# Merging the hi and lo halves of the moving operand into one wide matmul instruction in a float32 two-layer trunk

## The chip, the cores and the metric

One NeuronCore of a Trainium2 chip runs the whole kernel. The metric is device time of one execution in microseconds (us), the median of three runs. Engines are named as in the profile: PE (TensorE matmul), PEld (TensorE weight load), DVE (VectorE), ACT (ScalarE), POOL (GpSimd), SP (SyncE, which issues the transfers).

## The reference

A sequence of 256 tokens of 2048 features gets 16 meta tokens in front (272 in all, L) and runs through two layers, each `h <- h + norm(mixer(norm(h)))`. Layer 0 is differential attention with 8 heads: four projections (q, k, v and a gate), two score maps for each head (head dimension 128), two softmaxes over the allowed keys, `a = p1 - lam * p2`, values of 256 features, a norm for each head, a product with `silu(gate)`, an output projection. The queries are treated in three blocks: the 16 meta tokens (16 keys), the first 128 tokens (144 keys) and the second 128 tokens (272 keys). Layer 1 is a pooling mixer: a projection to u and a gate, causal window means of u minus u, a product with a 512 by 512 matrix in each of four feature groups (the mixing), a scale, a product with `silu(gate)`, an output projection. Everything is float32.

## The kernel before

Features lie on the 128 partitions and tokens along the free dimension. To hold float32 accuracy, each operand of a product is split in two float32r halves, hi (rounded) and lo (the exact rest). A product w x is then three matmuls that accumulate in one PSUM bank, `mm3` (lines 118 to 122): w_hi x_hi (L120), w_hi x_lo (L121), w_lo x_hi (L122), each with a weight load of its own. In the profile the weights are the stationary operand, and x's columns are the moving one.

Weights come as chunks of 128 by 2048 (1 MiB). `split` (L96 on ACT, L97 on DVE) makes hi and lo of a chunk; three places for each are in turn. One chunk of 128 output features is a *slot*: 16 contraction tiles, 48 matmuls (`proj`). In layer 0 the slots are q, q, k, k, v, v of each head, then 16 gate chunks. A head's attention runs between the projections of the next head, ordered by `after_proj`: at that head's first slot `scores` and `v_turn` (for head 0 a slot later, slot 7, and there ahead of the evacuation of the slot's own product), at its third `a_turn`, at its fourth `values`, at its fifth `sums` (L423, L424: sums of squares over partitions by a matmul with ones). In the fourth slot `qk_split` (L296 to L300) works on the same engines as the ending of `values`.

In `scores`, block 1 (first 128 queries, 144 keys) puts both maps in one bank and block 2 uses a bank for each map. DVE masks in place, takes the maximum, and ACT takes the exponential from PSUM (L377). In `values`, a bank gets one product for the meta keys (L411), an `mm3` of 256 columns and an `mm3` of 128 columns for the last key tile; ACT then squares (L414) and scales (L415) it, DVE adds the two squares (L416), ACT and DVE split the sum (L418, L419), and `sums` reads that.

In layer 1, `mixing` (L634) runs 16 `mm3` of 256 columns for each of four chunks, evacuated by one ACT instruction (L642). The 16 gate chunks (tile `pv`) are 16 `mm3` each of 256 columns, and `gate1` reads the bank with one DVE product (L646), then silu, product, split to zh and zl (L650). The output projection (tile `pz`) uses zh and zl as the stationary operand and 512 columns of weights as the moving one.

PSUM is one pool of eight banks for everything; a product waits until a bank is free. The order of instructions on an engine is fixed when the kernel is built, by a planner that goes by order in the program and by when it reckons an operand is ready; `tc.issue_after` adds a few orders by hand. The trace shows that it is not the bare program order: DVE's mask of block 1 (L371) stands among the small sums of block 0 (L346 to L348).

Of the kernel before, what the change touches and what calls it, by code (L numbers as in the profile page):

```python
# [42 lines left out]
def trunk(ctx: ExitStack, tc: tile.TileContext, hT, small, gpost1, rope, w_in, w_out, p_in, p_grp, p_out, out):  # L43
# [58 lines left out]
    def fold(f, o):  # L102
        """o = the sum of the KT tiles in f, which doesn't stay."""
# [14 lines left out]
    def mm3(o, wh, wl, xh, xl, first, last):  # L118
        """o += w^T x with both operands split; the product of the two low halves lies below float32's rounding."""
# [60 lines left out]
    xl = base.tile([P, KT, L], F32R, tag="xl", name="xl")  # L180
    oh = base.tile([P, KT, L], F32R, tag="oh", name="oh")
    ol = base.tile([P, KT, L], F32R, tag="ol", name="ol")
# [9 lines left out]
    # The first chunks run along with the loads of x, tile by tile.  # L192
# [63 lines left out]
    # Rope with the norm's factor in it: rp[:, 0] = r0 cos (1 beyond the rotated rows), rp[0:32, 1] = -+ r0 sin.  # L256
# [7 lines left out]
    # lambda = exp(q1 k1) - exp(q2 k2) + lambda_init, on every partition  # L264
# [7 lines left out]
    # sub-norm gain times (1 - lambda_init)  # L272
# [3 lines left out]
    def proj(ps, n0, n1, rh, rl, mid=None):  # L276
        """A chunk of 128 output features: ps[:, 0:n1-n0] over the tokens n0..n1."""
# [12 lines left out]
    def qk_evac(hd, i, ps):  # L290
        """i: q1, q2, k1, k2. Norm and the rope's cosine part; the swapped rows aside."""
# [13 lines left out]
    # The meta keys in one product: blocks of 32 partitions with v's (hi, hi, lo) against the weights' (hi, lo, hi);  # L305
    # the last 16 partitions of a block stay zero.
# [5 lines left out]
    def v_turn(hd):  # L312
        """v with the keys on the partitions, split; the norm's factor goes in here."""
# [18 lines left out]
    def scores(hd):  # L332
        """Softmaxes of both maps and their difference, by query block: hd.a[block], queries on the partitions."""
        h = hd.h
        hd.a = []
        for b, (q0, q1) in enumerate(TOK):
            nk, nq = q1, q1 - q0
            if b == 0:
                # Both maps' (hi, lo) queries against their (hi, lo) keys in one product, of which these parts count.
# [22 lines left out]
            mx = att.tile([P, 2], F32, name=f"mx{h}_{b}", tag=f"mx{b}")
            if b == 0:
# [10 lines left out]
            e = att.tile([P, 2, nk], F32, name=f"e{h}_{b}", tag=f"e{b}")  # L374
# [11 lines left out]
    def a_turn(hd):  # L386
        """The weights with the keys on the partitions, split."""
# [8 lines left out]
        hd.th = att.tile([P, 384], F32R, name=f"th{h}", tag="th")  # L396
        hd.tl = att.tile([P, 384], F32R, name=f"tl{h}", tag="tl")
# [6 lines left out]
    def values(hd):  # L404
        """The head's output, features on the partitions, and its squares."""
        h = hd.h
        hd.sq = att.tile([P, 2, L], F32, name=f"sq{h}", tag="e2")
        for j in range(2):
# [4 lines left out]
            mm3(po[:, 144:272], hd.vh[:, 1, s], hd.vl[:, 1, s], hd.th[:, 256:384], hd.tl[:, 256:384], False, True)  # L413
# [25 lines left out]
    def after_proj(slot, ps):  # L439
# [61 lines left out]
        # VectorE splits the next chunk before it turns to this one's products.  # L501
# [19 lines left out]
    for m in range(KT):  # L521
# [7 lines left out]
        if m >= KT - 5:  # L529
            # The next layer's first chunks run side by side: one more place for them.  # L530
# [34 lines left out]
    for n in (1, 1, 2, 2, 2, 2, 2, 2, 2):  # L565
        # h += norm(y) g; times the next norm's gain, split.
# [36 lines left out]
    # residual with the tokens on the partitions  # L603
# [198 lines left out]
```

## Time and profile before

| what | value |
|---|---|
| three runs | 852.3, 852.71, 853.0 us; median 852.71 |
| span of the profiled execution, first to last instruction | 850.4 us |
| median less that span | 2.3 us |
| granted TensorE clock, mean | 0.998 of full |
| PE busy | 838.5 us (99%), 6498 matmuls |
| DVE busy | 563.7 us (66%) |
| ACT busy | 420.9 us (49%) |
| DMA | 147.31 MB, mean 173 GB/s |
| chain that ended last | PE 96%, waiting for nothing shown 1%, the rest 1% or less each |

The time of the profiled execution is not listed apart from the three runs; what lies around its span is taken as the 2.3 us between span and median. A matmul's duration in the profile (some 280 ns for 256 columns) includes its way through the array, and matmuls overlap; what one costs in a row is the distance between the starts of two. The same holds for weight loads.

### The profile page before, as it was taken

The numbers are of one execution on the slowest core, as the hardware profiler recorded it, in microseconds if no ns is written. First come the engines' busy times: TensorE is split into PE (matmuls) and PEld (weight loads), VectorE is DVE, ScalarE is ACT, GpSimd is POOL, SyncE is SP. The second block draws the span as 40 slices with busy tenths as digits, with TensorE's granted clock in tenths as the row PEclk, the third lists the DMA queues.
The fourth block names the chain that finished last, engine by engine and source line by source line (L and its number), as shares of the span: only waits on it lengthen the run. The fifth ranks groups of instructions, "written<-read, shape, count | busy, mean of one in ns | idle before, by whom it ended". The sixth has DMA issues, their size and how long they took to land.

```text
span 850.4 us, 15239 instructions
## 1 busy us (share of the span) xinstructions
PE 838.5 (99%) x6498; PEld 823.1 (97%) x6498; DVE 563.7 (66%) x873; ACT 420.9 (49%) x617; POOL 5.4 (1%) x16
## 2 busy tenths in 40 slices
PE   8999999999999999999999999999999999999996
PEld 7999999999999999999999999999999999998896
DVE  6689676676758586977854454787767665574423
ACT  7556545454545455855343444554544444453420
POOL 0000000000000000000000000000000000000000
PEclk9999999999999999999999999999999999999999
DMA  8645444444444444445457546154575455546512
GB/s 298 218 158 190 149 149 150 150 148 162 144 179 149 161 149 150 149 153 194 155 199 298 198 153 241 54 201 151 193 249 188 164 195 198 178 169 202 194 50 99
DMA packets 24435, 147.31 MB, mean 173 GB/s; under 512 B 2736, under 2 KB 4528, under 8 KB 7856
## 3 DMA queue, kind: packets, MB, share of 16 engines
q1 hardware_dynamic: 24368, 146.34, 49.4%
q8 instruction: 51, 0.84, 0.4%
q14 instruction: 16, 0.13, 0.0%
HBM read 144.23 MB, written 2.10 MB: 172 GB/s over the span
## 4 chain that ended last, share of the span: by engine, by line
PE 96%; issue 1%; DMA 1%; DVE 1%; ACT 0%; SPq 0%; DVEq 0%; POOLq 0%; POOL 0%; ACTq 0%
PE p L120 14%; PE p L121 14%; PE p L122 14%; PE py L121 4%; PE py L120 4%; PE py L122 4%; PE pu L121 4%; PE pu L122 4%; PE pu L120 4%; PE pv L121 4%; PE pv L122 4%; PE pv L120 4%; PE pz L698 3%; PE pz L696 3%; PE pz L697 3%
## 5 line engine op out<-in xcount | busy, mean ns | idle before, releaser
L97 DVE TENSOR_TENSOR lo<-raw,hi 128x2048 fp32r<-128x2048 f32 (+1 forms) x126 | 281.8, 2238 | 156.2 <-ACT hi L96 155.9
L96 ACT CAST hi<-raw 128x2048 fp32r<-128x2048 f32 (+1 forms) x126 | 235.0, 1868 | 214.1 <-PE p L121 80.4
L120 PE MATMUL p<-xh,hi 128*128 128x272 f32 x944 | 274.2, 290 | 0.0
L121 PE MATMUL p<-xl,hi 128*128 128x272 f32 x944 | 273.1, 289 | 0.0
L122 PE MATMUL p<-xh,lo 128*128 128x272 f32 x944 | 272.6, 289 | 0.0
L120 PEld LDWEIGHTS p<-xh,hi 128*128 128x128 f32 x944 | 177.9, 188 | 0.0
L122 PEld LDWEIGHTS p<-xh,lo 128*128 128x128 f32 x944 | 177.7, 188 | 0.0
L121 PEld LDWEIGHTS p<-xl,hi 128*128 128x128 f32 x944 | 177.6, 188 | 0.0
L121 PE MATMUL py<-ol,hi 128*128 128x272 f32 x256 | 74.3, 290 | 0.0
L122 PE MATMUL py<-oh,lo 128*128 128x272 f32 x256 | 73.8, 288 | 0.0
L120 PE MATMUL py<-oh,hi 128*128 128x272 f32 x256 | 73.7, 288 | 0.0
L121 PE MATMUL pv<-hl,hi 128*128 128x256 f32 x256 | 72.1, 282 | 0.0
L122 PE MATMUL pv<-hh,lo 128*128 128x256 f32 x256 | 72.0, 281 | 0.0
L120 PE MATMUL pv<-hh,hi 128*128 128x256 f32 x256 | 71.6, 280 | 0.0
L122 PE MATMUL pu<-hh,lo 128*128 128x264 f32 (+3 forms) x192 | 54.6, 285 | 0.0
L121 PE MATMUL pu<-hl,hi 128*128 128x264 f32 (+3 forms) x192 | 54.6, 285 | 0.0
L120 PE MATMUL pu<-hh,hi 128*128 128x264 f32 (+3 forms) x192 | 54.3, 286 | 0.0
L122 PEld LDWEIGHTS pv<-hh,lo 128*128 128x128 f32 x256 | 48.5, 189 | 0.0
L120 PEld LDWEIGHTS pv<-hh,hi 128*128 128x128 f32 x256 | 48.4, 189 | 0.0
L120 PEld LDWEIGHTS py<-oh,hi 128*128 128x128 f32 x256 | 48.3, 189 | 0.0
L122 PEld LDWEIGHTS py<-oh,lo 128*128 128x128 f32 x256 | 48.2, 188 | 0.0
L121 PEld LDWEIGHTS pv<-hl,hi 128*128 128x128 f32 x256 | 48.0, 188 | 0.0
(228 smaller groups left out, 1430.5 us busy)
## 6 DMA issues: line engine op xcount, KB each, us to landing
raw<-in_w_in SPq DMA_DIRECT2D x60, 1024.0 KB, 4.9
raw<-in_p_in SPq DMA_DIRECT2D x32, 1024.0 KB, 4.9
raw<-in_w_out SPq DMA_DIRECT2D x16, 1024.0 KB, 4.9
raw<-in_p_out SPq DMA_DIRECT2D x14, 1024.0 KB, 4.8
raw<-in_p_grp SPq DMA_DIRECT2D x4, 1024.0 KB, 4.9
h<-in_hT SPq DMA_DIRECT2D x4, 544.0 KB, 7.3
raw<-in_w_in SPq DMA_DIRECT2D x4, 512.0 KB, 7.8
rawx<-in_p_out SPq DMA_DIRECT2D x2, 1024.0 KB, 6.0
```

The lines of the kernel that those rows point to most:

```text
L96: act.copy(hi[:, s], raw[i][:, s])
L97: rest[i] = dve.tensor_tensor(out=lw[:, s], in0=raw[i][:, s], in1=hi.bitcast(F32)[:, s], op=ALU.subtract)
L120: pe.matmul(o, wh, xh, start=first, stop=False)
L121: pe.matmul(o, wh, xl, start=False, stop=False)
L122: pe.matmul(o, wl, xh, start=False, stop=last)
L696: pe.matmul(ps, zh[:, k, s], wh[:, c], start=k == 0, stop=False)
L697: pe.matmul(ps, zh[:, k, s], wl[:, c], start=False, stop=False)
L698: pe.matmul(ps, zl[:, k, s], wh[:, c], start=False, stop=k == KT - 1)
```

## The change

A new helper `mm2` does the work of `mm3` with two matmuls: the first takes w_hi against x's hi and lo side by side (2n columns, two blocks of n in SBUF), into 2n columns of the bank; the second takes w_lo against x_hi into the first n columns. The columns n to 2n then hold w_hi x_lo, and have to be added by other engines. It is used where 2n is at most 512: the gate chunks and the mixing of layer 1 (n = 256), block 1 of the scores (n = 144), the last key tile of the values (n = 128). So that hi and lo lie side by side, xh and xl, oh and ol, hh and hl, zh and zl, mh and ml, eh and el, th and tl become the halves of one tile each. The score maps of block 1 take a bank each.

What is added on other engines: in `gate1` an ACT copy and a DVE sum of 256 columns a chunk; in `mixing` a DVE multiply-add of 256 columns for each output tile (the ACT instruction stays, on the other half); in block 1 of the scores an ACT copy and a DVE sum of 144 columns for each map (mask, maximum and exponential then work in SBUF on e); in `values` an ACT copy and a DVE sum in PSUM of 128 columns for each half, ahead of L414 and L415. Comments go too.

```diff
+    def mm2(ps, wh, wl, x, first, last):
+        n = x.shape[-1]
+        pe.matmul(ps[:, 0:2 * n], wh, x, start=first, stop=False, skip_group_check=not first)
+        pe.matmul(ps[:, 0:n], wl, x[:, 0], start=False, stop=last)
...
-    xh = base.tile([P, KT, L], F32R, tag="xh", name="xh")
...
+    xs = base.tile([P, 2, KT, L], F32R, tag="xs", name="xs")
+    os_ = base.tile([P, 2, KT, L], F32R, tag="os", name="os")
+    xh, xl, oh, ol = xs[:, 0], xs[:, 1], os_[:, 0], os_[:, 1]
...
-                pss = [bank(f"s{h}_{b}_{m}") for m in range(2)] if b == 2 else [bank(f"s{h}_{b}")] * 2
-                off = [0, 0 if b == 2 else 256]
+                pss = [bank(f"s{h}_{b}_{m}") for m in range(2)]
...
+                    if b == 1:
+                        mm2(pss[m], hd.qkh[:, m, qs], hd.qkl[:, m, qs], hd.qs[:, :, 2 + m, ks], True, True)
...
-                two = pss[0].rearrange("p (m k) -> p m k", m=2)
-                dve.memset(two[0:CHUNK, :, nk - CHUNK:nk], MASKED)
-                dve.reduce_max(mx[0:nq, :], two[0:nq, :, 0:nk], axis=AX.X)
+                for m in range(2):
+                    act.copy(e[:, m, :], pss[m][:, nk:2 * nk])
+                    dve.tensor_tensor(out=e[:, m, :], in0=S[m], in1=e[:, m, :], op=ALU.add)
+                S = [e[:, m, :] for m in range(2)]
+                dve.memset(e[0:CHUNK, :, nk - CHUNK:nk], MASKED)
+                dve.reduce_max(mx, e, axis=AX.X)
...
-            mm3(po[:, 144:272], hd.vh[:, 1, s], hd.vl[:, 1, s], hd.th[:, 256:384], hd.tl[:, 256:384], False, True)
+            mm2(po[:, 144:400], hd.vh[:, 1, s], hd.vl[:, 1, s], hd.t[:, :, 256:384], False, True)
+            act.copy(hd.sq[:, j, 144:272], po[:, 272:400])
+            dve.tensor_tensor(out=po[:, 144:272], in0=po[:, 144:272], in1=hd.sq[:, j, 144:272], op=ALU.add)
...
-                mm3(ps[:, 0:SEQ], wh[:, c:c + P], wl[:, c:c + P], zh[:, 4 * gi + k, :], zl[:, 4 * gi + k, :], k == 0, k == 3)
+                mm2(ps, wh[:, c:c + P], wl[:, c:c + P], zs[:, :, 4 * gi + k, :], k == 0, k == 3)
...
-            act.activation(mx[:, m, :], ps[:, 0:SEQ], AF.Copy, scale=sp[:, C_SCALE + m:C_SCALE + m + 1])
+            act.activation(mx[:, m, :], ps[:, SEQ:2 * SEQ], AF.Copy, scale=sc)
+            dve.scalar_tensor_tensor(out=mx[:, m, :], in0=ps[:, 0:SEQ], scalar=sc, in1=mx[:, m, :], op0=ALU.mult, op1=ALU.add)
...
-        dve.tensor_tensor(out=gs[:, 0:SEQ], in0=ps[:, 0:SEQ], in1=r1[:, NMETA:L], op=ALU.mult)
+        act.copy(gs[:, 0:SEQ], ps[:, SEQ:2 * SEQ])
+        dve.tensor_tensor(out=gs[:, 0:SEQ], in0=ps[:, 0:SEQ], in1=gs[:, 0:SEQ], op=ALU.add)
+        dve.tensor_tensor(out=gs[:, 0:SEQ], in0=gs[:, 0:SEQ], in1=r1[:, NMETA:L], op=ALU.mult)
...
-            proj(ps, NMETA, L, hh, hl)
+            wh, wl = take()
+            for k in range(KT):
+                mm2(ps, wh[:, k * P:(k + 1) * P], wl[:, k * P:(k + 1) * P], hs[:, :, k, NMETA:L], k == 0, k == KT - 1)
```

## Rows read from the trace of the kernel before

**Rows 1.** The page, busy us (share of the span) and instructions.

```profile
PE 838.5 (99%) x6498; PEld 823.1 (97%) x6498; DVE 563.7 (66%) x873; ACT 420.9 (49%) x617; POOL 5.4 (1%) x16
```

**Rows 2.** Busy us by stretch: one head (a_turn to a_turn), the gate chunks.

```profile
core 0: us, PE busy (x) PEld busy (x) DVE busy (x) ACT busy (x) POOL busy (x), PEclk, DMA share, GB/s
233.21:274.42 41.21, 41.21 (x330) 41.02 (x331) 28.55 (x58) 20.95 (x39) 0.00 (x0) 1.00 0.44 155
...
657.00:754.00 97.00, 97.00 (x821) 96.95 (x820) 59.66 (x70) 45.39 (x53) 0.00 (x0) 1.00 0.53 185
```

**Rows 3.** Timeline, PE, gate chunk: start us, us, engine, line; 171 steps.

```profile
682.75 0.28 PE L120 MATMUL pv<-hh,hi 128*128 128x256 f32 x1
...
702.99 0.28 PE L120 MATMUL pv<-hh,hi 128*128 128x256 f32 x1
```

**Rows 4.** Timeline, PE, one mixing chunk: its 48 matmuls, then the next.

```profile
596.33 0.28 PE L120 MATMUL pm<-zh,hi 128*128 128x256 f32 x1
...
602.08 0.29 PE L120 MATMUL pu<-hh,hi 128*128 128x264 f32 x1
```

**Rows 5.** Timeline, PE, output projection, 512 columns, 175 steps.

```profile
755.13 0.39 PE L696 MATMUL pz<-hi,zh 128*128 128x512 f32 x1
...
794.80 0.39 PE L697 MATMUL pz<-lo,zh 128*128 128x512 f32 x1
```

**Rows 6.** Timeline, weight loads: block 1's six, then block 2's first.

```profile
259.53 0.19 PEld L357 LDWEIGHTS s<-qs 128*128 128x128 f32 x1
...
260.20 0.19 PEld L357 LDWEIGHTS s<-qs 128*128 128x128 f32 x1
```

**Rows 7.** Timeline, weight loads: the last key tile's three, then the next projection's.

```profile
240.67 0.19 PEld L120 LDWEIGHTS o<-th,vh 128*128 128x128 f32 x1
...
241.02 0.19 PEld L120 LDWEIGHTS p<-xh,hi 128*128 128x128 f32 x1
```

**Rows 8.** Groups by line and shape: a DVE read of a gate bank.

```profile
L646 DVE TENSOR_TENSOR gs<-pv,r 128x256 f32<-128x256 f32 x16 | 6.8, 424 | 5.7 <-PE pv L122 5.7
```

**Rows 9.** Timeline, DVE: end of a head's softmax, and the last gate chunk's zl.

```profile
268.70 0.50 DVE L382 SCALAR_TENSOR_TENSOR a<-e,z 128x272 f32<-128x272 f32 x1 [0.17 <-ACT e L380]
...
760.52 0.42 DVE L650 TENSOR_TENSOR zl<-mx,zh 128x256 fp32r<-128x256 f32 x1
```

**Rows 10.** Timeline, DVE, one head's fourth and fifth slot, from values to sums.

```profile
241.93 2.27 DVE L97 TENSOR_TENSOR lo<-raw,hi 128x2048 fp32r<-128x2048 f32 x1
...
244.13 0.71 DVE L300 TENSOR_TENSOR qs<-qk,qs 128x544 fp32r<-128x544 f32 x1
...
244.77 0.42 DVE L416 TENSOR_TENSOR sq<-sq 128x272 f32<-128x272 f32 x1
...
245.68 0.44 DVE L419 TENSOR_TENSOR sh<-sq,sh 128x272 fp32r<-128x272 f32 x1 [0.49 <-ACT sh L418]
```

**Rows 11.** Timeline, ACT, the same stretch.

```profile
241.37 0.38 ACT L414 ACTIVATE sq<-o 128x272 f32<-128x272 f32 x1
...
242.03 0.40 ACT L414 ACTIVATE sq<-o 128x272 f32<-128x272 f32 x1
...
247.26 1.91 ACT L96 CAST hi<-raw 128x2048 fp32r<-128x2048 f32 x1 [1.61 <-PE p L121]
```

**Rows 12.** Timeline, PE, the same stretch: the first of the two sums.

```profile
247.18 0.29 PE L423 MATMUL sn<-sh,ones_r 128*128 128x272 f32 x1
```

**Rows 13.** Timeline, DVE, slot 7: last small sum of block 0, evacuation of p.

```profile
63.49 0.17 DVE L348 TENSOR_TENSOR s<-s,s 16x16 f32<-16x16 f32 x1
...
65.98 0.42 DVE L292 TENSOR_TENSOR qk<-p,rp 128x272 f32<-128x272 f32 x1
```

**Rows 14.** Timeline, ACT, slot 7: the chunk's split.

```profile
60.20 1.91 ACT L96 CAST hi<-raw 128x2048 fp32r<-128x2048 f32 x1 [0.94 <-DMA raw<-in_w_in]
```

**Rows 15.** Timeline, PE: first matmul after v_turn, in slot 7 and in a later head.

```profile
61.64 0.38 PE L120 MATMUL p<-xh,hi 128*128 128x272 f32 x1
...
261.63 0.37 PE L120 MATMUL p<-xh,hi 128*128 128x272 f32 x1
```

**Rows 16.** Timeline, DVE, the later head: evacuation of the slot's p.

```profile
260.10 0.46 DVE L293 STREAM_SHUFFLE sw<-p 32x272 f32<-32x272 f32 x1
```

More of the change, by code (lines that the diff above doesn't have):

```diff
@@ L178, in trunk @@
     r0 = const.tile([P, L], F32, name="r0")
-    xh = base.tile([P, KT, L], F32R, tag="xh", name="xh")
-    xl = base.tile([P, KT, L], F32R, tag="xl", name="xl")
-    oh = base.tile([P, KT, L], F32R, tag="oh", name="oh")
-    ol = base.tile([P, KT, L], F32R, tag="ol", name="ol")
+    xs = base.tile([P, 2, KT, L], F32R, tag="xs", name="xs")
+    os_ = base.tile([P, 2, KT, L], F32R, tag="os", name="os")
+    xh, xl, oh, ol = xs[:, 0], xs[:, 1], os_[:, 0], os_[:, 1]
     on = base.tile([P, KT, L], F32, tag="big", name="on")
@@ L350, in scores @@
             else:
-                pss = [bank(f"s{h}_{b}_{m}") for m in range(2)] if b == 2 else [bank(f"s{h}_{b}")] * 2
-                off = [0, 0 if b == 2 else 256]
+                pss = [bank(f"s{h}_{b}_{m}") for m in range(2)]
                 S = []
                 for m in range(2):
-                    o = pss[m][:, off[m]:off[m] + nk]
+                    o = pss[m][:, 0:nk]
                     qs, ks = slice(q0, q0 + P), slice(0, nk)
-                    pe.matmul(o, hd.qkh[:, m, qs], hd.qkh[:, 2 + m, ks], start=True, stop=False)
-                    pe.matmul(o, hd.qkh[:, m, qs], hd.qkl[:, 2 + m, ks], start=False, stop=False)
-                    pe.matmul(o, hd.qkl[:, m, qs], hd.qkh[:, 2 + m, ks], start=False, stop=True)
+                    if b == 1:
+                        mm2(pss[m], hd.qkh[:, m, qs], hd.qkl[:, m, qs], hd.qs[:, :, 2 + m, ks], True, True)
+                    else:
+                        pe.matmul(o, hd.qkh[:, m, qs], hd.qkh[:, 2 + m, ks], start=True, stop=False)
+                        pe.matmul(o, hd.qkh[:, m, qs], hd.qkl[:, 2 + m, ks], start=False, stop=False)
+                        pe.matmul(o, hd.qkl[:, m, qs], hd.qkh[:, 2 + m, ks], start=False, stop=True)
                     S.append(o)
             mx = att.tile([P, 2], F32, name=f"mx{h}_{b}", tag=f"mx{b}")
+            e = att.tile([P, 2, nk], F32, name=f"e{h}_{b}", tag=f"e{b}")
             if b == 0:
@@ L369, in scores @@
             else:
-                two = pss[0].rearrange("p (m k) -> p m k", m=2)
-                dve.memset(two[0:CHUNK, :, nk - CHUNK:nk], MASKED)
-                dve.reduce_max(mx[0:nq, :], two[0:nq, :, 0:nk], axis=AX.X)
+                for m in range(2):
[4 more added lines that the diff above has]
+                dve.reduce_max(mx, e, axis=AX.X)
             dve.tensor_scalar(out=mx[0:nq, :], in0=mx[0:nq, :], scalar1=-SCALE, scalar2=None, op0=ALU.mult)
-            e = att.tile([P, 2, nk], F32, name=f"e{h}_{b}", tag=f"e{b}")
             z = att.tile([P, 2], F32, name=f"z{h}_{b}", tag=f"z{b}")
@@ L395, in a_turn @@
         pe.transpose(pA[:, 144:272], hd.a[2][:, 0:P], ident)
-        hd.th = att.tile([P, 384], F32R, name=f"th{h}", tag="th")
-        hd.tl = att.tile([P, 384], F32R, name=f"tl{h}", tag="tl")
+        hd.t = att.tile([P, 2, 384], F32R, name=f"t{h}", tag="t")
+        hd.th, hd.tl = hd.t[:, 0], hd.t[:, 1]
         act.copy(hd.th, pB[:, 0:384])
@@ L537, in trunk @@
                 load(IU + m - KT + 5)
-    hh = base.tile([P, KT, L], F32R, tag="xh", name="hh")
-    hl = base.tile([P, KT, L], F32R, tag="xl", name="hl")
+    hs = base.tile([P, 2, KT, L], F32R, tag="xs", name="hs")
+    hh, hl = hs[:, 0], hs[:, 1]
     r1 = l1.tile([P, L], F32, name="r1")
@@ L587, in trunk @@
     cur[0] += 1
-    mh = base.tile([P, 2, CW], F32R, tag="oh", name="mh")
-    ml = base.tile([P, 2, CW], F32R, tag="ol", name="ml")
+    ms = base.tile([P, 2, 2, CW], F32R, tag="os", name="ms")
+    mh, ml = ms[:, 0], ms[:, 1]
     with tc.issue_after(hhs[9].ins):
@@ L613, in trunk @@
     mx = base.tile([P, KT, SEQ], F32, tag="big", name="mx")
-    zh = base.tile([P, KT, SEQ], F32R, tag="oh", name="zh")
-    zl = base.tile([P, KT, SEQ], F32R, tag="ol", name="zl")
+    zs = base.tile([P, 2, KT, SEQ], F32R, tag="os", name="zs")
+    zh, zl = zs[:, 0], zs[:, 1]
     def pooled(t, ps):
@@ L639, in mixing @@
                 c = k * 512 + j * P
-                mm3(ps[:, 0:SEQ], wh[:, c:c + P], wl[:, c:c + P], zh[:, 4 * gi + k, :], zl[:, 4 * gi + k, :], k == 0, k == 3)
+                mm2(ps, wh[:, c:c + P], wl[:, c:c + P], zs[:, :, 4 * gi + k, :], k == 0, k == 3)
             m = 4 * gi + j
-            act.activation(mx[:, m, :], ps[:, 0:SEQ], AF.Copy, scale=sp[:, C_SCALE + m:C_SCALE + m + 1])
+            sc = sp[:, C_SCALE + m:C_SCALE + m + 1]
+            act.activation(mx[:, m, :], ps[:, SEQ:2 * SEQ], AF.Copy, scale=sc)
+            dve.scalar_tensor_tensor(out=mx[:, m, :], in0=ps[:, 0:SEQ], scalar=sc, in1=mx[:, m, :], op0=ALU.mult, op1=ALU.add)
     def gate1(t, ps):
         gs = l1.tile([P, L], F32, tag="u", name=f"gs1_{t}", bufs=2)
-        dve.tensor_tensor(out=gs[:, 0:SEQ], in0=ps[:, 0:SEQ], in1=r1[:, NMETA:L], op=ALU.mult)
+        act.copy(gs[:, 0:SEQ], ps[:, SEQ:2 * SEQ])
+        dve.tensor_tensor(out=gs[:, 0:SEQ], in0=ps[:, 0:SEQ], in1=gs[:, 0:SEQ], op=ALU.add)
+        dve.tensor_tensor(out=gs[:, 0:SEQ], in0=gs[:, 0:SEQ], in1=r1[:, NMETA:L], op=ALU.mult)
         act.activation(gs[:, 0:SEQ], gs[:, 0:SEQ], AF.Silu)
@@ L718, in out_store @@
             nc.sync.dma_start(out[b * P:(b + 1) * P, c], ht[:, b, c])
-    eh = base.tile([P, 2, CW], F32R, tag="xh", name="eh")
-    el = base.tile([P, 2, CW], F32R, tag="xl", name="el")
+    es = base.tile([P, 2, 2, CW], F32R, tag="xs", name="es")
+    eh, el = es[:, 0], es[:, 1]
     for n in range(3):
```

## The prediction

> **What bounds the kernel now.** I read the page first, for who is busy: PE 99% of the span, DVE 66%, ACT 49% [rows 1]. Then the busy times by stretch, for whether the other two come near PE anywhere that the change touches: in one head of 41.21 us DVE works 28.55 and ACT 20.95, over the gate chunks of 97.00 us DVE 59.66 and ACT 45.39, at the full granted clock [rows 2]. So PE sets the time in both stretches, and time is won there only by fewer or shorter steps of PE, while work given to DVE and ACT costs nothing until PE has to wait for its result or for a bank that it still holds. Last the timeline of PE, for the step from one matmul to the next: that, and not the duration in the profile, is what an instruction costs.
>
> A step of 256 columns in the gate chunks is (702.99 - 682.75) / 171 = 118.4 ns [rows 3], in the mixing 5.75 / 48 = 119.8 ns [rows 4], of 512 columns 39.67 / 175 = 226.7 ns [rows 5]. Twice the columns is not twice the time: between 118.4 and 226.7 a column costs 0.423 ns, and some 10 ns hang on the instruction. For narrow matmuls the columns don't count at all: six matmuls of 144 columns take 0.67 us from weight load to weight load, 112 ns each [rows 6], where 0.423 x 144 + 10 would be 71; three of 128 columns take 0.35, 117 each [rows 7]. There the distance of the weight loads is the limit.
>
> **What it removes, part by part.** *Gate chunks:* 16 chunks x 16 contraction tiles, each time two steps of 256 become one of 512 and the third stays: 2 x 118.4 - 226.7 = 10.1 ns, x 256 = 2.6 us. *Mixing:* 4 chunks x 16, 2 x 119.8 - 226.7 = 12.9 ns, x 64 = 0.8 us. *Scores, block 1:* 8 heads x 2 maps; three steps at 112 = 336 become one of 288 columns, 118.4 + 32 x 0.423 = 132, and one of 144 at 112: 92 ns less, x 16 = 1.5 us. *Values, last key tile:* 16 times, three steps of 350 in all become one of 256 (118) and one of 128 (112 to 117): 0.12 us less, x 16 = 1.9 us. Sum 6.8 us of PE time.
>
> The merged instruction reads two blocks of columns a whole tile half apart; the 512 columns of [rows 5] are one block. No row shows a wide one of two blocks. If the second block cost the fixed part again, gate and mixing would win nothing; if the fixed part were that of the mixing, the gate would win 3.3. I take 10.1 because the columns stream at one rate in all rows, and keep 0 and 12.9 as ends.
>
> The Trainium skill, TensorE: Matmul & The Clock Gate, section Back-to-back issue gap, gives a warm step as N / 2.4 + 2.5 ns. By it 512 columns would take 216 ns and 256 columns 109; the trace has 226.7 and 118.4 and disagrees, so I go by the rows. By the page a merged pair would save 2.5 ns, gate and mixing together 0.8 us instead of 3.4, and the sum would be 4.2.
>
> **What it adds, and what hides it.** A DVE instruction over 256 columns takes 0.42 us [rows 8]; one over 128 or 144 lies between 0.17 (16 columns, [rows 13]) and 0.42, and I use 0.25; the ACT copies I put at 0.3, below the 0.38 of a 272-column square [rows 11]. Each gate chunk gets 0.42 on DVE and about 0.4 on ACT in a slot of some 5.5 us of which DVE was idle 38% [rows 2]; each mixing chunk gets 4 x 0.42 on DVE, which has only a split to do under it. A head gets about 1 us on each, of 12.7 and 20.3 idle [rows 2]. Three places have a deadline.
>
> *The softmax.* Block 1 gets two copies and two sums ahead of its maximum, some 1.2 us. In the head shown the last weights are ready at 269.20 [rows 9] and a_turn starts at 274.42, the border of the head's stretch [rows 2]: 5.2 us of cover, so nothing. *The last gate chunk.* Its zl ends at 760.94 [rows 9]; the output projection begins at about 754 [rows 2] and reads tile 15 after 72 steps of 226.7, at 770.2: 9 us of cover for 0.9.
>
> *Values to sums.* This one is short. Now the head's squares are split by 245.68 + 0.44 = 246.12 [rows 10], and the sums start at 247.18 [rows 12]: 1.06 us. With the change the square (L414) waits for a DVE sum in PSUM. ACT has the copies done before 242.0, but DVE then runs a chunk's lo until 244.20 and L300 until 244.84 [rows 10]. If the sums stand behind both, the first ends about 245.1; ACT's square, scale and square take 242.03 + 0.40 - 241.37 = 1.06 [rows 11]; L416 starts at 246.2 instead of 244.77 and L419 ends at 247.5 instead of 246.12: PE waits about 0.37 us. Behind the waiting `sn` stand the next slot's projection and all of PE. This pattern holds for six heads (head 0 has its sums under a slot without `qk_split`, head 7 a slot later): 2.2 us. If the planner puts the sums ahead of the lo, or moves `sn` among the next projection's matmuls, 0. I take half, 1.1.
>
> *Banks.* `scores` and `v_turn` now hold seven of the eight banks instead of six, with the slot's own p in the eighth, so the next projection waits for a release. In heads 1 to 7 p is evacuated at once, at 260.56 [rows 16], and the next projection starts at 261.63 [rows 15], 0.2 earlier after the change: 0.9 us of cover. In slot 7 (once) p is evacuated only from 65.98 [rows 13], the projection wants its bank at 61.64 [rows 15], and the first releases are block 1's, after ACT's split ends at 62.11 [rows 14] and a copy and a sum (about 62.9), or block 0's, at 63.66 [rows 13]. That is a wait of 0 (if the copies come ahead of the split) to 2.2 us; I take 1.2.
>
> Merging hi and lo tiles makes some tiles free only when both halves are. The last reader of both was the same product before (L121 and L122 of one `mm3`), so that costs nothing. Transfers are the same.
>
> **Sum.** 6.8 - 1.1 - 1.2 = 4.5 us less. The span goes from 850.4 to 845.9; with the 2.3 us around it, that is 848.2 against the median of 852.7.
>
> **Rivals.** *No wait at all:* both covers hold. For it speaks that the planner reorders DVE already. 852.7 - 6.8 = 845.9. *Both waits in full:* 6.8 - 2.2 - 2.2 = 2.4 won, 850.3.
>
> *Two blocks cost as two instructions*, so that the change saves no fixed part: gate and mixing win 0, scores and values still lose a weight load each and 10 ns less, 3.1, less 2.3 of waits: 851.9, no change. Nothing in the trace speaks for it but that such an instruction isn't in it.
>
> *A fixed part of 2.5 ns*, that is, most of the 10 ns belongs to something that the merged pair keeps: 4.2 less 2.3 of waits, 850.8. This is what the rule of the Trainium skill's page named above makes of the sum; [rows 3] and [rows 5] speak against it.
>
> *Slower: the head's split of the squares falls behind the next chunk's hi.* ACT starts that hi at 247.26 and is held by it for 1.91 us [rows 11]. By the working above L416 ends at 246.6, so the cast L418 precedes it by 0.65 us. If the planner puts the hi first, L418 runs from 249.2, L419 ends at 250.0, and PE waits 2.9 us a head, 17 us for six: 852.7 - 6.8 + 17.2 + 1.2 = 864.3. It decides from a wait of 1.1 us a head on, which eats the 6.8. For it: a static order and a long instruction that is ready early; against it: that hi's place comes free only with the projection's last matmuls, at about 247.
>
> **How the numbers follow.** Forecast (some wait in both places, 846.5 to 850): 0.47. No wait 0.18, full waits 0.09, two blocks as two 0.10, fixed part 2.5 ns 0.04, slower 0.12. About 0.2%, 1.7 us, is what a measurement can tell from no change. Faster by more: 0.47 + 0.18 + 0.09 + 0.04 = 0.78; the same 0.10; slower 0.12. The range runs from the gate at 12.9 ns without waits (845.2, with a little room) up over the two-block case and some more wait: 844.5 to 853.0, which leaves out the slower case.
>
> **What the profile after would show.** The gate chunks: a pair of steps of 227 and 118 where three of 118 stood; if the first is 237, the two blocks cost twice, if it is under 225 the gain is larger. Block 1's weight loads: two in 0.24 us for each map. PE at `sn` in six heads: a gap of 0 to 0.4 us, or 3 if the slower case holds; DVE's lo between ACT's copy and DVE's sum would be its cause. PE after the first `v_turn`: a gap of about 1 us, released by DVE. Wrong it would be by a wait on PE of over 1 us that comes back in each head or each gate chunk, such as a bank held by an evacuation behind a split.

## The result

The changed kernel takes 847.55 us (median of four runs, 847.45 to 848.33) against 852.86 us (four runs, 852.3 to 853.06): ratio 0.9939, 95% interval 0.9927 to 0.9951, so 4.2 to 6.2 us faster. The forecast was 848.2 us, and faster.

The page of the changed kernel: PE has 352 matmuls and 4.4 us less, DVE 15.9 and ACT 10.9 us more than in [rows 1].

```profile
PE 834.1 (99%) x6146; PEld 805.2 (95%) x6146; DVE 579.6 (68%) x937; ACT 431.8 (51%) x665; POOL 5.4 (1%) x16
```

Its busy times by stretch, one head from `a_turn` to `a_turn`. The stretch is 0.39 us shorter than the head in [rows 2], PE still fills it, and DVE and ACT have 11.7 and 19.0 us to spare.

```profile
core 0: us, PE busy (x) PEld busy (x) DVE busy (x) ACT busy (x) POOL busy (x), PEclk, DMA share, GB/s
232.31:273.13 40.82, 40.82 (x327) 40.63 (x326) 29.12 (x61) 21.85 (x43) 0.00 (x0) 1.00 0.45 156
```

Its timeline of PE, in order of time: the first projection of slot 5; slot 7; the first of the sums; one mixing chunk and the matmul behind it; the third gate chunk's first pair and the first matmul of the output projection. The name in brackets is what ended PE's idle time.

```profile
42.16 0.37 PE L120 MATMUL p<-xs,hi 128*128 128x272 f32 x1
...
62.30 0.27 PE L324 MATMUL vA<-ident,vT 128*128 128x128 f32 x1
62.90 0.39 PE L120 MATMUL p<-xs,hi 128*128 128x272 f32 x1 [0.33 <-DVE e L381]
...
246.67 0.29 PE L436 MATMUL sn<-sh,ones_r 128*128 128x272 f32 x1
...
594.64 0.39 PE L128 MATMUL pm<-zs,hi 128*128 128x512 f32 x1
...
600.18 0.29 PE L120 MATMUL pu<-hs,hi 128*128 128x264 f32 x1
...
671.63 0.40 PE L128 MATMUL pv<-hs,hi 128*128 128x512 f32 x1
671.86 0.28 PE L129 MATMUL pv<-hs,lo 128*128 128x256 f32 x1
...
749.87 0.39 PE L715 MATMUL pz<-hi,zs 128*128 128x512 f32 x1
```

The stretch of the same 14 gate chunks in the timeline of PE before:

```profile
674.23 0.28 PE L120 MATMUL pv<-hh,hi 128*128 128x256 f32 x1
...
753.75 0.40 PE L696 MATMUL pz<-hi,zh 128*128 128x512 f32 x1
```

*Mixing:* 5.54 us for a chunk that took 5.75 [rows 4]; the four chunks fall from 23.0 to 22.3 us. *Gate:* 14 chunks of 16 pairs lie between 671.63 and 749.87, 78.24 / 224 = 349.3 ns a pair, where the same stretch before, 674.23 to 753.75, makes 79.52 / 224 = 355.0. Taken apart over all 16 chunks, a wide step has a mean of 230.8 ns and a low one 118.4. *Slot 7:* the projection starts 0.60 us after the last transpose, some 0.11 of which is that transpose's own step. *Sums:* `sn` follows the projection with no idle time.

Its weight loads: block 1's first and block 2's first.

```profile
259.02 0.19 PEld L128 LDWEIGHTS s<-qs 128*128 128x128 f32 x1
...
259.50 0.19 PEld L365 LDWEIGHTS s<-qs 128*128 128x128 f32 x1
```

Four loads in 0.48 us, two in 0.24 for each map, where six took 0.67 [rows 6].

Its timeline of DVE, in slot 7 and from `values` to `sums`:

```profile
62.56 0.28 DVE L381 TENSOR_TENSOR e<-s,e 128x144 f32<-128x144 f32 x1
...
62.85 0.29 DVE L381 TENSOR_TENSOR e<-s,e 128x144 f32<-128x144 f32 x1
...
241.62 0.48 DVE L426 TENSOR_TENSOR o<-o,sq 128x128 f32<-128x128 f32 x2
242.02 2.27 DVE L97 TENSOR_TENSOR lo<-raw,hi 128x2048 fp32r<-128x2048 f32 x1
244.22 0.71 DVE L306 TENSOR_TENSOR qs<-qk,qs 128x544 fp32r<-128x544 f32 x1
...
245.77 0.44 DVE L432 TENSOR_TENSOR sh<-sq,sh 128x272 fp32r<-128x272 f32 x1 [0.48 <-ACT sh L431]
```

Its timeline of ACT, at the same two places:

```profile
60.91 0.53 ACT L380 COPY e<-s 128x144 f32<-128x144 f32 x2 [0.67 <-PE s L129]
...
241.07 0.42 ACT L425 COPY sq<-o 128x128 f32<-128x128 f32 x2
...
245.31 0.42 ACT L431 CAST sh<-sq 128x272 fp32r<-128x272 f32 x1 [1.60 <-DVE sq L429]
246.74 1.91 ACT L96 CAST hi<-raw 128x2048 fp32r<-128x2048 f32 x1 [1.01 <-PE p L121]
```

The planner put the two new DVE sums (L426) ahead of the chunk's lo (L97). The split of the squares ends at 246.21, 0.46 us before `sn` wants it; before the change it was 1.06 (246.12 against 247.18, [rows 10, 12]). So no head waits there, but more than half of the cover is gone. In slot 7 PE is released by DVE's sum of block 1, which stood behind a lo and a copy of block 0 and began at 62.56.

The start-up is noise in every comparison: slot 5's first projection begins at 40.87 to 42.16 us in the profiled executions, latest in this one of the changed kernel (42.16; before 41.30). Its span of 846.5 us is therefore too long by 0.9 us beside the 850.4 of before. The table therefore counts from that matmul to the end. Each ratio is to runs of the kernel before that were timed beside that kernel (their medians are 852.5 to 852.9 us).

| kernel | median us | ratio to before, 95% interval | profiled span | slot 5 begins | from there to the end |
|---|---|---|---|---|---|
| before | 852.86 | | 850.43 | 41.30 | 809.14 |
| changed | 847.55 | 0.9939, 0.9927 to 0.9951 | 846.53 | 42.16 | 804.37 |
| e1 gate alone | 850.66 | 0.9974, 0.9964 to 0.9984 | 848.87 | 41.21 | 807.66 |
| e2 mixing alone | 852.01 | 0.9992, 0.9983 to 1.0001 | 850.00 | 41.64 | 808.36 |
| e3 scores and values alone | 849.36 | 0.9959, 0.9947 to 0.9972 | 847.75 | 41.11 | 806.64 |
| e4 no bank wait | 847.12 | 0.9931, 0.9918 to 0.9943 | 845.34 | 41.41 | 803.93 |
| e5 sums late | 854.99 | 1.0026, 1.0016 to 1.0035 | 853.41 | 41.17 | 812.24 |
| e6 adjacent | 847.95 | 0.9945, 0.9930 to 0.9960 | 846.64 | 40.91 | 805.73 |
| e7 padded | 847.12 | 0.9934, 0.9917 to 0.9950 | 846.56 | 41.52 | 805.04 |
| e8 cast late | 876.31 | 1.0278, 1.0257 to 1.0298 | 874.64 | 40.87 | 833.78 |
| e9 two wide | 875.87 (one run) | | 874.10 | 41.10 | 833.00 |
| e10 zigzag | 847.75 | 0.9939, 0.9926 to 0.9953 | 845.66 | 41.49 | 804.17 |
| e11 bank and pad | 846.62 | 0.9926, 0.9912 to 0.9939 | 845.03 | 41.25 | 803.79 |
| e12 row moving | 847.68 (one run) | | 845.91 | 40.91 | 804.99 |

### The profile page after: what moved, and what is told of

Its sections match the earlier page's. It is cut to its first block, busy times and chain, and to the rows that moved or that the text cites. A ratio compares the mean times of both kernels' runs of the same rounds, so it can differ in the third digit from the quotient of the medians.

```text
span 846.5 us, 14624 instructions
## 1 busy us (share of the span) xinstructions
PE 834.1 (99%) x6146; PEld 805.2 (95%) x6146; DVE 579.6 (68%) x937; ACT 431.8 (51%) x665; POOL 5.4 (1%) x16
## 4 chain that ended last, share of the span: by engine, by line
PE 91%; DVE 2%; DMA 2%; issue 2%; ACT 1%; SPq 0%; DVEq 0%; POOLq 0%; POOL 0%; ACTq 0%
PE p L120 13%; PE p L121 13%; PE p L122 13%; PE pv L128 7%; PE py L121 4%; PE py L120 4%; PE py L122 4%; PE pu L121 4%; PE pu L122 4%; PE pu L120 4%; PE pv L129 4%; PE pz L717 3%; PE pz L715 3%; PE pz L716 3%; PE pm L128 2%
## 5 line engine op out<-in xcount | busy, mean ns | idle before, releaser
L97 DVE TENSOR_TENSOR lo<-raw,hi 128x2048 fp32r<-128x2048 f32 (+1 forms) x126 | 281.6, 2237 | 148.5 <-ACT hi L96 148.2
L120 PE MATMUL p<-xs,hi 128*128 128x272 f32 x944 | 274.2, 290 | 0.3 <-DVE e L381 0.3
L121 PE MATMUL p<-xs,hi 128*128 128x272 f32 x944 | 273.2, 289 | 0.0
L122 PE MATMUL p<-xs,lo 128*128 128x272 f32 x944 | 272.6, 289 | 0.0
L120 PEld LDWEIGHTS p<-xs,hi 128*128 128x128 f32 x944 | 177.9, 188 | 0.6 <-DVE e L381 0.6
L122 PEld LDWEIGHTS p<-xs,lo 128*128 128x128 f32 x944 | 177.6, 188 | 0.0
L121 PEld LDWEIGHTS p<-xs,hi 128*128 128x128 f32 x944 | 177.5, 188 | 0.0
L128 PE MATMUL pv<-hs,hi 128*128 128x512 f32 x256 | 89.5, 393 | 0.0
L121 PE MATMUL py<-os,hi 128*128 128x272 f32 x256 | 74.3, 290 | 0.0
L122 PE MATMUL py<-os,lo 128*128 128x272 f32 x256 | 73.8, 288 | 0.0
L120 PE MATMUL py<-os,hi 128*128 128x272 f32 x256 | 73.7, 288 | 0.0
L129 PE MATMUL pv<-hs,lo 128*128 128x256 f32 x256 | 71.8, 280 | 0.0
L128 PEld LDWEIGHTS pv<-hs,hi 128*128 128x128 f32 x256 | 48.1, 188 | 10.9
L121 PE MATMUL pu<-hs,hi 128*128 128x264 f32 (+3 forms) x192 | 54.5, 285 | 0.0
L120 PE MATMUL pu<-hs,hi 128*128 128x264 f32 (+3 forms) x192 | 54.4, 287 | 0.0
L120 PEld LDWEIGHTS py<-os,hi 128*128 128x128 f32 x256 | 48.3, 189 | 0.0
L121 PEld LDWEIGHTS py<-os,hi 128*128 128x128 f32 x256 | 48.0, 188 | 0.0
```

The source lines that it names most:

```text
L120: pe.matmul(o, wh, xh, start=first, stop=False)
L121: pe.matmul(o, wh, xl, start=False, stop=False)
L122: pe.matmul(o, wl, xh, start=False, stop=last)
L128: pe.matmul(ps[:, 0:2 * n], wh, x, start=first, stop=False, skip_group_check=not first)
L129: pe.matmul(ps[:, 0:n], wl, x[:, 0], start=False, stop=last)
```

## The experiments

### The parts alone: e1, e2, e3

Each takes one part of the change and leaves the others as before. e1 keeps only the gate:

```diff
-                mm2(ps, wh[:, c:c + P], wl[:, c:c + P], zs[:, :, 4 * gi + k, :], k == 0, k == 3)
+                mm3(ps[:, 0:SEQ], wh[:, c:c + P], wl[:, c:c + P], zh[:, 4 * gi + k, :], zl[:, 4 * gi + k, :], k == 0, k == 3)
...
-            mm2(po[:, 144:400], hd.vh[:, 1, s], hd.vl[:, 1, s], hd.t[:, :, 256:384], False, True)
+            mm3(po[:, 144:272], hd.vh[:, 1, s], hd.vl[:, 1, s], hd.th[:, 256:384], hd.tl[:, 256:384], False, True)
...
-                pss = [bank(f"s{h}_{b}_{m}") for m in range(2)]
+                pss = [bank(f"s{h}_{b}")] * 2 if b == 1 else [bank(f"s{h}_{b}_{m}") for m in range(2)]
```

> Only layer 1's gate takes the 512-column product; mixing, block 1's scores and the last value tile are as before. Theory of the trace after (a wide step of about 230.8 ns and a low step of 118.3 ns, so 5.7 ns a triple): 1.4 us less than the kernel before, near 851.4 us, and the stretch of 14 gate chunks falls from 79.5 to about 78.2 us. The prediction's own term (226.7 ns, 10.1 ns a triple): 2.6 us less, near 850.2 us, with the stretch at 77.2 us. Rival, the extra copy and sum of each chunk bind: no gain, 852.8 us, the stretch at 79.5 us.

Its timeline of PE: slot 5, the third gate chunk, the output projection.

```profile
41.21 0.37 PE L120 MATMUL p<-xs,hi 128*128 128x272 f32 x1
...
673.96 0.40 PE L128 MATMUL pv<-hs,hi 128*128 128x512 f32 x1
...
752.18 0.39 PE L718 MATMUL pz<-hi,zs 128*128 128x512 f32 x1
```

The 14 chunks take 78.22 us, as in the changed kernel. From slot 5 on the run is 1.5 us shorter than before. The median fell by 2.2, with an interval of 1.4 to 3.1 us; the interval alone would allow the prediction's 2.6, the timeline doesn't.

e2 keeps only the mixing; the gate goes back like this, the rest as in e1:

```diff
-                mm2(ps, wh[:, k * P:(k + 1) * P], wl[:, k * P:(k + 1) * P], hs[:, :, k, NMETA:L], k == 0, k == KT - 1)
+            proj(ps, NMETA, L, hh, hl)
```

> Only mixing takes the 512-column product. Theory: its 64 triples fall from about 359.7 to 348 ns, 0.74 us less, near 852.1 us. The prediction's term was 0.83 us. Rival, the evacuation in two instructions (ScalarE, then VectorE) delays what follows: the four groups keep their 23.0 us or the gap moves behind them, 852.8 us.

Its timeline of PE, the first mixing chunk and the matmul behind it:

```profile
596.66 0.39 PE L128 MATMUL pm<-zs,hi 128*128 128x512 f32 x1
...
602.21 0.29 PE L120 MATMUL pu<-hs,hi 128*128 128x264 f32 x1
```

5.55 us, and 0.8 less from slot 5 on: the mixing's term stands, and the evacuation in two steps delays nothing.

e3 takes both of those back and keeps scores and values:

```diff
-                mm2(ps, wh[:, c:c + P], wl[:, c:c + P], zs[:, :, 4 * gi + k, :], k == 0, k == 3)
+                mm3(ps[:, 0:SEQ], wh[:, c:c + P], wl[:, c:c + P], zh[:, 4 * gi + k, :], zl[:, 4 * gi + k, :], k == 0, k == 3)
...
+            proj(ps, NMETA, L, hh, hl)
```

> Only block 1's scores and the last value tile are merged; gate and mixing are as before. Theory: 0.39 us in each of 8 heads, 3.1 us, less one wait of about 0.6 us in slot 7, so 2.5 us less, near 850.3 us; the head's period 40.8 us. The prediction's terms (3.4 us of work less 1.1 us at the sums and 1.2 us in slot 7): 1.1 us less, near 851.7 us, and the period with the wait at the sums would be above 41.0 us in six heads.

Its timeline of PE: slot 5, and slot 7 behind the last transpose.

```profile
41.11 0.37 PE L120 MATMUL p<-xs,hi 128*128 128x272 f32 x1
...
61.95 0.39 PE L120 MATMUL p<-xs,hi 128*128 128x272 f32 x1 [0.43 <-DVE e L381]
```

2.5 us less from slot 5 on, a head's period of 40.81 to 40.82, and the wait in slot 7 again. The three parts come to 1.5 + 0.8 + 2.5 = 4.8, and the whole gave 4.8 by the same count: they add.

### The wait for a bank: e4

```diff
+                one = b == 1 and h == 0
-                pss = [bank(f"s{h}_{b}_{m}") for m in range(2)]
+                pss = [bank(f"s{h}_{b}")] * 2 if one else [bank(f"s{h}_{b}_{m}") for m in range(2)]
...
-                    if b == 1:
+                    if b == 1 and not one:
```

> The changed kernel, with head 0's block 1 scores alone as before (three products for each map, both maps in one bank); the other seven heads stay merged. Theory: the gap of about 0.6 us before the last product of slot 8 goes, the head loses 0.18 us of merged scores, so 0.4 us less than the changed kernel, near 847.1 us. Rival, the gap comes from the general crowding of slot 7 and not from the bank: it stays, and the time is that of the changed kernel or 0.2 us more.

Its timeline of PE in slot 7:

```profile
61.73 0.27 PE L324 MATMUL vA<-ident,vT 128*128 128x128 f32 x1
61.76 0.38 PE L120 MATMUL p<-xs,hi 128*128 128x272 f32 x1
```

The idle time is gone: it was the eighth bank. 0.4 us less than the changed kernel from slot 5 on, and 0.4 in the medians. The times alone could not tell that from nothing; the timeline does. Head 0's scores in three matmuls cost it 2 x 92 ns, so the wait was worth 0.6.

### The order that the planner chose: e5 and e8

In e5 the two DVE sums of `values`, and what follows from them, are issued a slot later and behind the chunk's lo:

```diff
-            dve.tensor_tensor(out=po[:, 144:272], in0=po[:, 144:272], in1=hd.sq[:, j, 144:272], op=ALU.add)
-            act.square(hd.sq[:, j, :], po[:, 0:L])
...
     def sums(hd):
+        for j, po in enumerate(hd.po):
+            with tc.issue_after(rest[cur[0] + 1].ins):
+                dve.tensor_tensor(out=po[:, 144:272], in0=po[:, 144:272], in1=hd.sq[:, j, 144:272], op=ALU.add)
+            act.square(hd.sq[:, j, :], po[:, 0:L])
...
```

> The changed kernel with the two DVE sums of the values (and the squares, scales and split that follow from them) put by hand behind the next chunk's lo, as the prediction feared the planner would do it. Theory (the prediction's working of this order): PE waits about 0.37 us at the first matmul of the sums in six heads, 2.2 us in all, near 849.8 us, and the head's period goes from 40.81 to about 41.2 us. Rival, the cover of 0.46 us that the trace after shows is enough in this order too: the period stays at 40.8 and the time at 847.5 us.

Its timeline of DVE in a head, from values to sums:

```profile
242.33 2.27 DVE L97 TENSOR_TENSOR lo<-raw,hi 128x2048 fp32r<-128x2048 f32 x1
...
245.17 0.48 DVE L433 TENSOR_TENSOR o<-o,sq 128x128 f32<-128x128 f32 x2
...
247.58 0.44 DVE L439 TENSOR_TENSOR sh<-sq,sh 128x272 fp32r<-128x272 f32 x1 [0.49 <-ACT sh L438]
```

Its timeline of PE, the sums of that head and of the last one:

```profile
247.24 0.29 PE L122 MATMUL p<-xs,lo 128*128 128x272 f32 x1
247.60 0.40 PE L441 MATMUL sn<-sh,ones_r 128*128 128x272 f32 x1
...
380.51 0.60 PE L441 MATMUL sn<-sh,ones_r 128*128 128x272 f32 x1 [2.76 <-ACT sh L438]
```

Its busy times behind the wait in the last head (columns as above):

```profile
380.50:383.50 3.00, 2.99 (x13) 3.00 (x14) 2.34 (x3) 0.60 (x2) 0.00 (x0) 0.50 0.21 33
```

This is slower than the kernel before. `sn` could have followed the projection's last matmul at about 247.36; the cast that it waits for is done only after the sums have waited for the lo, and the split ends at 248.02. The period of heads 1 to 6 goes from 40.82 to 41.38 us: 0.56 a head, 3.4 in all, where the forecast had 0.37 a head. Another 4.5 us come from the last head, which the forecast had not priced: there ACT's cast of the squares fell behind a chunk's hi, PE stood for 2.76 us, and for 3 us after that the granted clock was 0.50, the lower of the two levels (1.2 GHz): 13 matmuls in 3 us. That is the order of the prediction's slower rival, once.

e8 forces this rival in every head: the cast of the summed squares stands behind the hi of the chunk after next.

```diff
+        split(cur[0] + 2)
+        with tc.issue_after(his[cur[0] + 2].ins):
+            act.copy(hd.sh[:, 0, :], hd.sq[:, 0, :])
+        dve.tensor_tensor(out=hd.sh[:, 1, :], in0=hd.sq[:, 0, :], in1=hd.sh.bitcast(F32)[:, 0, :], op=ALU.subtract)
         ps = bank(f"sn{hd.h}")
```

> The changed kernel with ACT's cast of the head's summed squares put behind the hi of the chunk after next, the order of the prediction's slower rival, in all eight heads. By that rival's working PE waits 2.4 to 2.9 us a head: 19 to 23 us more than the changed kernel, 867 to 871 us, and a period of 43.2 to 43.7 us. If PE finds other work in that time, less: the period stays below 41.8 us and the time below 856 us.

Its waits of PE: what waited for what, us in total, times, longest.

```profile
PE sn L438 <- ACT sh L435: 19.8, 8, 2.5
```

Its busy times behind the waits of two heads:

```profile
218.50:221.00 2.50, 2.50 (x21) 2.50 (x22) 1.95 (x3) 0.00 (x0) 0.00 (x0) 1.00 0.03 3
...
262.00:264.50 2.50, 2.50 (x11) 2.50 (x12) 1.91 (x2) 0.00 (x0) 0.00 (x0) 0.50 0.00 0
```

29.4 us more than the changed kernel from slot 5 on, above the 19 to 23 expected. The eight waits are alike (2.5 us each, 19.8 in all), but behind five of them (heads 0, 2, 4, 6 and 7) the granted clock is 0.50 for some 3 us, as at 262, and behind three it is not, as at 218.5. What decides between the two, these runs do not show. A head costs 2.7 us more without the fall and 4.1 to 4.3 with it. The Trainium skill, TensorE: Matmul & The Clock Gate, section HAM oscillation — how this bites in real kernels, tells of a kernel that waited some 3 to 5 us for a transfer at every tile and came back from each wait at the slow clock. The waits here are shorter, 2.5 us, and only five of the eight came back slow.

### What makes the wide step 231 ns: e6, e7, e9, e10, e12

The forecast took the 226.7 ns of [rows 5] for the wide step of the gate; it measured 230.8. Five kernels looked for the 4 ns.

e6 puts the hi and lo of a tile side by side, so that the mixing reads one unbroken block:

```diff
-    zs = base.tile([P, 2, KT, SEQ], F32R, tag="os", name="zs")
+    zs = base.tile([P, KT, 2, SEQ], F32R, tag="os", name="zs")
...
-    hs = base.tile([P, 2, KT, L], F32R, tag="xs", name="hs")
+    hs = base.tile([P, KT, 2, L], F32R, tag="xs", name="hs")
```

> The changed kernel with the hi and lo of one tile next to each other: in the mixing the 512 moving columns are one unbroken block (before: two blocks 16 KiB apart), in the gate the two blocks of 256 are 16 columns apart (before: 17 KiB). Theory, a far second block costs the 4 us-thousandths that the wide step takes more than the 226.7 ns of an unbroken one: the wide step falls from 230.8 to about 227 ns, the gate's 16 chunks from 89.4 to about 88.4 us and the mixing from 22.3 to 22.0, together 1.3 us less, near 846.3 us. Rival, the steps vary by a few ns with the place of the operands whatever the distance of the two blocks: the mean of a triple stays between 346 and 352 ns in both, no change beyond 0.5 us.

Its timeline of PE, the second mixing chunk:

```profile
619.58 0.39 PE L128 MATMUL pm<-zs,hi 128*128 128x512 f32 x1
...
625.13 0.29 PE L120 MATMUL pu<-hs,hi 128*128 128x272 f32 x1
```

5.55 us, where the changed kernel with its two blocks 16 KiB apart has 5.55 too (619.51 to 625.06); the four chunks take 22.4 us against 22.3, and a gate pair 350.0 ns. So two blocks cost no more than one unbroken block (the mixing), nor far ones more than near ones (the gate).

e7 moves the rows:

```diff
-    hs = base.tile([P, 2, KT, L], F32R, tag="xs", name="hs")
+    hs = base.tile([P, 2, KT, 276], F32R, tag="xs", name="hs")[:, :, :, 0:L]
```

> The changed kernel with rows of 276 instead of 272 tokens in layer 1's hi and lo tile (four unused columns behind each row): the two blocks stay about as far apart, only the places of the rows change. Theory, the steps depend on the place of the operands: the triples of a gate chunk, which now take 344 to 360 ns in a pattern that comes back every eight contraction tiles, take another pattern, and the mean of 349.3 may move by some ns (1 us in all for 4 ns). Rival, the distance of the blocks alone: pattern and mean stay, 89.4 us for the gate, 847.5 us.

The pair's pattern over the contraction tiles changed, its mean hardly: 348.8 ns (349.3), 0.1 us for the gate. The place of the rows moves single steps by up to some 10 ns and nearly cancels in a sum of sixteen. This execution lost more than that elsewhere. Its busy times early in layer 1, where in the changed kernel the clock stays at 1.00:

```profile
536.05:538.05 2.00, 2.00 (x12) 2.00 (x11) 1.74 (x5) 0.57 (x2) 0.00 (x0) 0.50 0.00 0
```

The granted clock fell during the norm between the layers, and the way from that norm's first matmul to the first mixing chunk took 63.0 instead of 61.9 us (63.3 in e6, where it fell too). e11 has the same rows and no fall there, so the fall is not the padding's.

e9 makes all of the gate's instructions wide, so that the width never changes from one matmul to the next:

```diff
-                mm2(ps, wh[:, k * P:(k + 1) * P], wl[:, k * P:(k + 1) * P], hs[:, :, k, NMETA:L], k == 0, k == KT - 1)
+                x = hs[:, :, k, NMETA:L]
+                pe.matmul(ps, wh[:, k * P:(k + 1) * P], x, start=k == 0, stop=False)
+                pe.matmul(ps, wl[:, k * P:(k + 1) * P], x, start=False, stop=k == KT - 1)
```

> The changed kernel with the gate's second instruction made 512 columns wide too (lo weights against hi and lo of x, so the product of the two low halves comes in as well). It tells where the wide step's 230.8 ns come from. Theory, a change of width from one matmul to the next costs some 4 ns: with all of one width the step falls to the 226.7 ns of the output projection, a chunk's pair to 453 ns, the 16 chunks to 116.1 us, 26.7 us more than the changed kernel. Rival, the moving operand (two blocks of tokens instead of a row of weights) makes the wide step 230.8 ns wherever it stands: a pair takes 461.6 ns, the 16 chunks 118.2 us, 28.8 us more.

Its timeline of PE, third gate chunk to output projection:

```profile
674.02 0.40 PE L692 MATMUL pv<-hs,hi 128*128 128x512 f32 x1
...
777.43 0.40 PE L717 MATMUL pz<-hi,zs 128*128 128x512 f32 x1
```

103.41 / 448 = 230.8 ns for each wide step: the change of width is not it. The same is seen from the other side in e10, which turns the order round at every second tile:

```diff
+                if k % 2:
+                    pe.matmul(ps[:, 0:SEQ], wl[:, s], x[:, 0], start=False, stop=False)
+                    pe.matmul(ps, wh[:, s], x, start=False, stop=k == KT - 1)
+                else:
+                    mm2(ps, wh[:, s], wl[:, s], x, k == 0, False)
```

> The changed kernel with the gate's wide and low instruction in turned order at every second contraction tile (wide, low, low, wide), so that the width changes half as often. Theory, the change of width costs some 4 ns: a triple falls from 349.3 to about 347 ns, the 16 chunks from 89.4 to 88.9 us, 0.5 us less in all. Rival, the moving operand: the mean stays at 349.3 ns within 1 ns, no change.

Its timeline of PE, the same stretch:

```profile
670.97 0.40 PE L128 MATMUL pv<-hs,hi 128*128 128x512 f32 x1
...
749.00 0.40 PE L720 MATMUL pz<-hi,zs 128*128 128x512 f32 x1
```

78.03 / 224 = 348.3 ns a pair, 1 ns less where 2.3 were expected of a cost by width.

e12 lets the gate's wide instruction read an unbroken row of the chunk's lo instead of x:

```diff
-                mm2(ps, wh[:, k * P:(k + 1) * P], wl[:, k * P:(k + 1) * P], hs[:, :, k, NMETA:L], k == 0, k == KT - 1)
+                pe.matmul(ps, wh[:, k * P:(k + 1) * P], wl[:, j:j + 512], start=k == 0, stop=False)
+                pe.matmul(ps[:, 0:SEQ], wl[:, k * P:(k + 1) * P], x[:, 0], start=False, stop=k == KT - 1)
```

> The changed kernel, but the gate's wide instruction takes 512 columns of the chunk's own lo row as the moving operand, in place of x's hi and lo (so the gate's values are not the reference's; count, shapes and weight loads are the same). Theory, the moving operand makes the difference between the gate's 230.8 ns and the output projection's 226.7: the wide step falls to about 227 ns, a triple to 345, the 16 chunks from 89.4 to 88.4 us. Rival, the stationary operand does (a slice of a weight chunk here, of zh there): the step stays at 230.8 ns, the chunks at 89.4 us.

Its timeline of PE, the same stretch:

```profile
670.46 0.40 PE L693 MATMUL pv<-lo,hi 128*128 128x512 f32 x1
...
749.23 0.40 PE L718 MATMUL pz<-hi,zs 128*128 128x512 f32 x1
```

78.77 / 224 = 351.7 ns, longer and not shorter: the theory that the moving operand explains the 4 ns falls. Distance, change of width and kind of the moving operand are excluded. The mixing's wide steps, taken apart like the gate's, have a mean of 231.7 ns, so the excess is not the gate's alone. What is left is the weights that are loaded (a slice of a weight chunk in the gate, of zh in the output projection, where two matmuls in a row load the same one) or the places of the operands. The runs don't settle it.

### The best of it: e11

```diff
+                one = b == 1 and h == 0
...
-    hs = base.tile([P, 2, KT, L], F32R, tag="xs", name="hs")
+    hs = base.tile([P, 2, KT, 276], F32R, tag="xs", name="hs")[:, :, :, 0:L]
```

> The changed kernel with head 0's block 1 as before (no wait for a bank in slot 7) and layer 1's rows padded to 276 tokens. Theory: the two effects add, 0.4 us from the bank, 0.2 us in gate and mixing and 0.45 us in the u projections, so 1.1 us less than the changed kernel, near 846.5 us, if the clock isn't lowered behind the second norm as in the run with padded rows (1.2 us). Rival: they don't, 847.5 us.

846.62 us, the lowest median of the study. From slot 5 on it is 0.6 us shorter than the changed kernel and 0.1 shorter than e4, so most of it is the bank. The 0.45 us that I had put down to the u projections were none: in e7 those steps looked shorter because PE came to them late, behind the slow clock, and so missed the wait near their start in the changed kernel (one step of 500 ns among those of 120).

## Why the prediction was right

| term | predicted us | measured us | from |
|---|---|---|---|
| gate | 2.6 | 1.5 | e1; 256 x 5.7 ns by the pairs |
| mixing | 0.8 | 0.7 | the four chunks, 23.0 to 22.3 us; e2 has 0.8 |
| scores and values | 3.4 | 3.1 | 8 x 0.39, the head's period; e3's 2.5 and the bank's 0.6 |
| wait at the sums | -1.1 | 0 | timeline, no idle time |
| wait for the bank | -1.2 | -0.6 | e4 |
| net | 4.5 | 4.8 | slot 5 to the end |

The mechanism was right: PE bounds every stretch, fewer instructions and weight loads shorten it, and the copies and sums cost nothing where DVE and ACT had room. That the net came out nearly exact is luck, since two errors offset each other: 1.5 us less won than forecast, 1.7 us less waited. The case that was given the best chance had some wait in both places; only the bank's came.

*The term that was mis-sized* is the gate's, 10.1 ns a pair. It took the wide step from the output projection [rows 5]; in the gate it is 230.8 ns, and a merged pair saves 2 x 118.4 - 230.8 = 6 ns by the steps and 5.7 by the pairs. The result lies inside the prediction's ends of 0 and 12.9. "If the second block cost the fixed part again, gate and mixing would win nothing" is out: both won, and in e6 the mixing's unbroken block costs what its two blocks do. Nearly half of the gate's gain went all the same, and what the wide step spends its 4 ns on is open. The Trainium skill, TensorE: Matmul & The Clock Gate, section Back-to-back issue gap, gives N / 2.4 + 2.5 ns as the gap of an isolated matmul, and an estimate from it is 2.5 ns a pair. The gate's 5.7 and the mixing's 11 ns (0.7 us over 64 pairs) disagree with it.

*The mixing's* size came out by luck too: its wide step is 231.7 ns, 5 longer than taken, but its low step 116.7, 3 shorter than the 119.8 that the forecast kept. That leaves 11 of the 12.9 ns.

*Scores and values:* two weight loads in 0.24 us for a map, as forecast; 0.39 us a head where the sum of the two terms is 0.42.

*The wait at the sums:* the prediction said that the planner decides and took half. The planner put the sums ahead of the lo, which is the 0 of its two ends. The price of the other order was too low: 0.56 us a head in place of 0.37, and 4.5 us in the last head, for which the forecast had no wait. The rival with "full waits" stood at 850.3 us; e5, which has that order, took 855.0, more than the kernel before.

*The bank:* the place and the releaser were right, DVE's sum of block 1. It came sooner than taken because ACT's copies went ahead of the chunk's split (60.91 against 61.33). The prediction gave a wait of 0 for that order, and there it was wrong: DVE's sum still stood behind a lo, and PE waited.

*The slower rival* did not happen, but it is real: e5 shows it in one head and e8 in eight. Its wait was priced at 2.9 us a head and measured 2.5 (2.7 by the period); what it left out is the fall of the clock, with which a head loses 4.2.

*No visible cost* in the softmax, the last gate chunk and the shared tiles, as forecast: from the first mixing chunk on, the time saved is that of gate and mixing, 155.2 us to the output projection (594.64 to 749.87) against 157.4 (596.33 to 753.75), and the output projection and what follows take 96.7 us in both.

## What to carry to other kernels

Where PE bounds a stretch, merging two products that share their weights is worth what the timeline shows from start to start of such instructions, in that very place: here 6 to 11 ns where two products of 256 columns became one, but about 100 ns where two of 128 or 144 did, since there the step was the distance of the weight loads, 112 to 117 ns [rows 6, 7]. The copies and sums that this needs were free here because they stood ahead of the long splits on DVE and ACT, and not behind them (e5); put the order down by hand when the gain rests on it, since here one order gave 5 us and the other took 2. Count the banks that a wider result holds, above all where the evacuation comes late.

## What the runs showed that I had not expected

A wait of PE can have a second price. Behind a wait of 2.5 us the granted clock was 0.50 for about 3 us in five cases of eight, worth another 1.4 us; the same kernel at the same line shows both outcomes (e8). In the norm between the layers, where one step takes 0.6 us in all of them, it fell in e6 and e7 and not in the changed kernel or e11, for 1.2 to 1.4 us.

Matmuls of one shape don't take one time: in the gate a wide step lasts 225 to 235 ns and a low one 113 to 125, in a pattern that comes back in each chunk and moves with the row length (e7). With hi and lo of a tile side by side (e6) the pattern all but goes, most wide steps 231 or 233 ns and most low ones 118, and the pair costs the same. A term of 10 ns an instruction is as small as that spread.
